# An encoder layer on one core: row sums paused and then run at another pace, decay tables held back, out weights fetched a unit sooner with low weights first, x stored in halves

## The chip, the cores and the metric

The kernel runs on one core of a Trainium2 chip. Its time is the device time of one execution in microseconds (us). Three executions took 1106.18, 1106.75 and 1107.64 us; the median, 1106.75, is the time before. A change of less than about 0.2% of that can't be told from none.

The engines in the text: PE is TensorE (matrix multiplications and transposes), DVE is VectorE, ACT is ScalarE, POOL is GpSimd, SP is SyncE, which issues almost all DMA transfers. Each works through its own queue in order.

## What is computed

One encoder layer for two sequences of 512 rows of 1024 numbers, called the prompt (b = 0) and the sample (b = 1), in float32:

```
mod = silu(c) @ w_ada + b_ada                    # six vectors: sh1, sc1, g1, sh2, sc2, g2
h = rms_norm(x) * (1 + sc1) + sh1
q_a, k_a, v_a, q_r, k_r, v_r, g_r = split(h @ w_in)
o_a = windowed_attention(q_a, k_a, v_a, sink)    # 8 heads of 64, |t - s| <= 128, 2 key/value heads
o_r = silu(g_r) * group_norm(retention(q_r, k_r, v_r, decays))   # 4 heads of 128, both directions
x = x + g1 * (concat(o_a, o_r) @ w_out)
h = rms_norm(x) * (1 + sc2) + sh2
x = x + g2 * (square(relu(h @ w_mlp1)) @ w_mlp2)
y = rms_norm(x, final_g)
```

## The kernel before

**Precision and the matmul.** PE multiplies in a rounded 32-bit format (fp32r). Every operand is split: a high part, rounded by ACT (`split_high`, line 93), and a low part, the difference, taken by DVE (line 101). A product is then three matmuls: high by high, high by low, low by high. In tile names the letters `wh` and `wl` stand for the high and the low part of a weight, followed by the matrix: `rv`, `rq`, `rk`, `rg` for the retention's values, queries, keys and gates, `wo` for the out projection. `mm3_late` (lines 131, 132 and 134) issues the three for a group of banks at once, with the third, the one that needs the late operand, at the end of the group. For the out projection the late operand is the low weight.

**Stages.** The first 48 us are a front whose order is written out by hand: loads, the first modulation vectors, the first norm, and the projections of the prompt's attention. Then come lists of units. A unit loads one weight tile (`load`, always one unit ahead of its use) and multiplies (`use`). `run_units` walks a list. After each group of matmuls a unit yields, and between the two the scheduler of the kernel (`between(rate)`) lets other work in: pieces of attention and retention for which the operands are ready (the `rate` says how many), and, at the pace `clock[3]`, one step of `background_mods`. The lists in order: the prompt's retention values (4 units) and its four retention heads (3 units each), the sample's attention, values and heads, the prompt's out projection (8 units: two halves `hf` of the output columns, four slices `kq` of the input), the sample's out projection, and from 511 us on the MLP's products.

**The background.** 60 row sums on DVE (line 178, `reduce_unit`): a 128 by 1024 tile of w_ada times the activated condition vector, which lies in the tile `cb`, summed along the row. They give the parts of `mod` that the front has not computed: those of the sample's first norm, then gates and the second norm's. Each has its place in DVE's queue fixed behind the last instruction before it. What is left of them when the prompt's out projection has been issued is run in one go (`while background`).

**The late pool.** Then `mixer.close()` gives the memory of one pool (`cb`, attention's and retention's tables) free, and the pool `late` is opened on it. The sample's out projection takes its low weights `wl_wo` from `late` (three buffers), its high weights from the ordinary weight buffers. Both were stored to DRAM by the prompt's units (`kept_wo`, line 110) and are loaded from there (line 119).

**The out projection's end.** For each of four row tiles `t` the product `po_hf_t` is multiplied by the gate (`go`, line 782) and added to x (line 783). The tile x is loaded when the first half is done (line 780) and, when the second is, stored to the DRAM tensor `x2s` (`store`, line 728) for the layer's end; its squares are summed (line 723), and it is scaled in place by its norm's factor (lines 742 and 744), for which the store has to have read it. PE then transposes it (`px`, line 268). In a name such as po_1_3 the first number is the half, the second the row tile; the last number of a name is a running number and means nothing.

**The decay tables.** `decay_table` (line 529 and the two behind it) makes a 128 by 896 table for each retention head of the prompt: ACT scales a table of distances, DVE takes a minimum, ACT exponentiates. It is needed by the first score block of that head; two buffers take turns.

**What sets the order.** Within the lists a scheduler places instructions by their operands and by the order in which the program issues them; two helpers bind it: `issue_after(i)` keeps what follows behind instruction i on its engine, and `keep_in_program_order` keeps a transfer behind the ones that the program issued before it.

## Time and profile before

| what | value |
|---|---|
| median of three executions | 1106.75 us (1106.18 to 1107.64) |
| the profiled execution | 1105.71 us, of which the span of the records is 1103.9 us |
| granted clock of TensorE | 0.998 of full speed, mean |
| PE busy | 1078.9 us (98%) |
| DVE busy | 864.6 us (78%) |
| ACT busy | 515.9 us (47%) |
| moved by DMA | 232.73 MB, 211 GB/s on average |

In a profile row of the timeline the first number is the start and the second the duration in us, then engine, line, operation, the tile written, an arrow and the tiles read, then shapes; what stands in square brackets is how long the engine had been idle before and what ended that. Rows of the waits view read: engine, its operation and line, what it waited for; then total, number of times and the longest. SPq is SP's queue: a row is the issue of a transfer, not its duration. Matmul records overlap: one of 128 by 512 lasts 0.39 us in the records, and the next starts 0.227 us after it.

### The profile page before, as it was taken

What the parts mean: (1) busy time and instruction counts of PE and PEld (TensorE: products, weight loads), DVE (VectorE), ACT (ScalarE), POOL (GpSimd) and SP (SyncE); (2) the same over time, 40 slices, a digit from 0 to 9 for tenths busy, and PEclk for the clock granted to TensorE, in tenths of its full rate; (3) what the DMA queues carried; (4) which work ended last, traced back from release to release, by engine and by line L of the source; (5) the groups of instructions that cost most, each with busy time, mean ns of one, the idle gap of its engine ahead of it and who ended that gap; (6) DMA issues with size and microseconds to landing.
All of it is one profiled execution on the core that took longest, in us unless ns stands there. A gap on an engine that the chain in (4) does not pass through costs nothing.

```text
span 1103.9 us, 14022 instructions
## 1 busy us (share of the span) xinstructions
PE 1078.9 (98%) x5021; PEld 888.9 (81%) x5021; DVE 864.6 (78%) x1448; ACT 515.9 (47%) x885; POOL 49.0 (4%) x55
## 2 busy tenths in 40 slices
PE   7999999999999999999999999999999999999997
PEld 5777788778888788888888888888788888888886
DVE  7979989877887787889878777886659754589786
ACT  6576666545653433574333343333443733335342
POOL 1000000000000001000000000000000000002213
PEclk9999999999999999999999999999999999999999
DMA  9889698765545698734546444452883556525504
GB/s 374 334 301 322 248 379 289 234 194 176 181 139 191 233 360 300 274 123 139 189 169 198 155 162 166 169 181 105 307 322 106 187 194 203 198 77 191 191 19 153
DMA packets 86746, 232.73 MB, mean 211 GB/s; under 512 B 8578, under 2 KB 20882, under 8 KB 86676
## 3 DMA queue, kind: packets, MB, share of 16 engines
q1 hardware_dynamic: 86084, 231.25, 60.2%
q8 instruction: 39, 0.64, 0.2%
q10 hardware_dynamic: 432, 0.57, 0.1%
q14 instruction: 31, 0.25, 0.1%
q0 software_dynamic: 160, 0.02, 0.0%
HBM read 160.75 MB, written 71.06 MB: 210 GB/s over the span
## 4 chain that ended last, share of the span: by engine, by line
PE 87%; DVE 8%; ACT 2%; DMA 1%; issue 1%; POOL 0%; POOLq 0%; ACTq 0%; DVEq 0%
PE x L1350 16%; PE px_None L933 15%; PE y L1350 12%; PE py_None L933 11%; PE po L132 3%; PE po L134 3%; PE po L131 3%; PE po L393 2%; PE ppt L386 2%; PE psc L360 1%; PE pj_rq L131 1%; PE pj_rq L132 1%; PE pj_rq L134 1%; PE pj_rg L134 1%; PE pj_rk L132 1%; PE pj_rk L131 1%
## 5 line engine op out<-in xcount | busy, mean ns | idle before, releaser
L1290 DVE TENSOR_TENSOR uc_l<-ur,uc_h 128x1024 fp32r<-128x1024 f32 x56 | 68.4, 1221 | 53.1 <-ACT uc_h L1290 36.0
L1350 PE MATMUL x<-wc_h,uc_h 128*128 128x512 f32 (+1 forms) x264 | 100.9, 383 | 0.7 <-ACT adacc L246 0.7
L1350 PE MATMUL x<-wc_l,uc_h 128*128 128x512 f32 (+1 forms) x264 | 101.0, 383 | 0.0
L1350 PE MATMUL x<-wc_h,uc_l 128*128 128x512 f32 (+1 forms) x264 | 101.0, 383 | 0.0
L1290 ACT CAST uc_h<-ur 128x1024 fp32r<-128x1024 f32 x56 | 58.9, 1051 | 77.3 <-PE x L1350 25.1
L1350 PE MATMUL y<-wc_h,uc_h 128*128 128x512 f32 x192 | 74.7, 389 | 0.0
L1350 PE MATMUL y<-wc_l,uc_h 128*128 128x512 f32 x192 | 74.7, 389 | 0.0
L1350 PE MATMUL y<-wc_h,uc_l 128*128 128x512 f32 x192 | 74.7, 389 | 0.0
L1290 ACT CAST wc_h<-w 128x1024 fp32r<-128x1024 f32 x48 | 50.5, 1051 | 48.1 <-PE x L1350 24.7
L1290 DVE TENSOR_TENSOR wc_l<-w,wc_h 128x1024 fp32r<-128x1024 f32 x48 | 58.6, 1220 | 17.6 <-ACT wc_h L1290 13.8
L1350 PEld LDWEIGHTS x<-wc_h,uc_h 128*128 128x128 f32 x264 | 49.6, 188 | 10.9 <-ACT adacc L246 1.2
L1350 PEld LDWEIGHTS x<-wc_h,uc_l 128*128 128x128 f32 x264 | 49.6, 188 | 9.8
L1350 PEld LDWEIGHTS x<-wc_l,uc_h 128*128 128x128 f32 x264 | 49.6, 188 | 9.6
L131 PE MATMUL po<-wh_wo,ms 128*128 128x512 f32 x128 | 50.2, 396 | 0.0
L132 PE MATMUL po<-wh_wo,ms 128*128 128x512 f32 x128 | 49.8, 392 | 0.1
L178 DVE CUSTOM_DVE_ANT_0 jka_b<-raw_adat,cb,cols 128x1024 bf16<-128x1024 f32 x38 | 48.2, 1279 | 0.1
L838 ACT CAST wc_s4h<-raw_w 128x1024 fp32r<-128x1024 f32 x16 | 16.8, 1052 | 63.1 <-PE px_None L933 54.1
L370 ACT ACTIVATE st<-st,negm 128x256 f32<-128x256 f32 (+1 forms) x64 | 35.2, 554 | 15.6 <-DVE negm L365 15.6
L1350 PEld LDWEIGHTS y<-wc_h,uc_l 128*128 128x128 f32 x192 | 36.0, 188 | 7.5
L1350 PEld LDWEIGHTS y<-wc_h,uc_h 128*128 128x128 f32 x192 | 36.0, 188 | 7.5
L1350 PEld LDWEIGHTS y<-wc_l,uc_h 128*128 128x128 f32 x192 | 36.0, 188 | 7.5
L933 PE MATMUL py_None<-hch,wc_a 128*128 128x512 f32 x120 | 39.7, 389 | 0.0
(378 smaller groups left out, 2954.8 us busy)
## 6 DMA issues: line engine op xcount, KB each, us to landing
ur<-spill SPq DMA_DIRECT2D x56, 512.0 KB, 4.5
raw_adat<-in_w_ada_t_dram SPq DMA_DIRECT2D x36, 512.0 KB, 6.9
raw_w<-in_w_mlp_dram SPq DMA_DIRECT2D x32, 512.0 KB, 3.5
spill<-s SPq DMA_DIRECT2D x64, 256.0 KB, 3.7
w<-in_w_mlp_dram SPq DMA_DIRECT2D x32, 512.0 KB, 5.2
spill<-u SPq DMA_DIRECT2D x48, 256.0 KB, 2.0
raw_ada<-in_w_ada_t_dram SPq DMA_DIRECT2D x12, 512.0 KB, 9.3
x<-in_x_dram SPq DMA_DIRECT2D x12, 512.0 KB, 7.2
```

Of the source, the lines that this page charges most:

```text
L131: nc.tensor.matmul(ps, lhs[0], rhs[0], start=start, stop=False)
L132: nc.tensor.matmul(ps, lhs[late], rhs[1 - late], start=False, stop=False)
L134: nc.tensor.matmul(ps, lhs[1 - late], rhs[late], start=False, stop=stop)
L178: nc.vector.tensor_tensor_reduce(junk(f"jka_{name}_{sec}_{kc}_{b}"), t, cb[:, b, :], 1.0, bcol[:, sec * KC + kc:sec * KC + kc + 1] if bias ...
L360: nc.tensor.matmul(psc[:, :w], qs[hh][:, isl], k_[:, s, j0 * P:j1 * P], start=(s == 0), stop=(s == 1))
L370: nc.scalar.activation(st[hh][:, :w], st[hh][:, :w], AF.Exp, bias=negm[:, hh:hh + 1], scale=0.125, accum_out=den[:, hh:hh + 1])
L386: nc.tensor.transpose(pt[:, hh * P:(hh + 1) * P], st[hh][:, jj * P:(jj + 1) * P], ident)
L393: nc.tensor.matmul(po, va[:, j0 + jj, g].rearrange("p s e -> p (s e)"), pts[jj][:, s, :], start=(jj == 0 and s == 0), stop=(jj == nj - 1 a ...
L838: nc.scalar.copy(hi, src)
L933: self.last = nc.tensor.matmul(bank[:, cs], x[:, k, :], y, start=first and k == 0 and i == 0, stop=last and k == 3 and i == 2, skip_group_ ...
L1290: last_split[:] = [nc.scalar.copy(hi, src), nc.vector.tensor_sub(lo, src, f(hi))]
L1350: nc.tensor.matmul(out, left[n][x][:, i, ts_], right[n][y][:, i, cs], start=first and i == 0 and k == 0, stop=end and i == 1 and k == 2, s ...
```

## The change

Five pieces:

1. The first ACT instruction of a decay table is held behind the ACT instruction issued last before it.
2. The first `run_units` starts with pace 0.0, and a hook behind its fourth unit sets the pace to 0.8 (it was 0.7 from the start). So no row sum runs beside the four value units.
3. The sample's list of units and the prompt's out projection become one list, run at rate 1.3 (the out projection was a list of its own at rate 1.0). So the first out weight is loaded during the last retention unit.
4. In the sample's out projection `mm3_late` issues the low weights' matmuls first instead of last.
5. The sample's x tiles are stored in two halves, each right behind its own add into x.

```diff
--- before.py
+++ after.py
@@ -125,13 +125,18 @@
         nc.tensor.matmul(ps, lhs[0], rhs[1], start=False, stop=False)
         nc.tensor.matmul(ps, lhs[1], rhs[0], start=False, stop=stop)
 
-    def mm3_late(groups, late):
-
-        for ps, lhs, rhs, start, _ in groups:
-            nc.tensor.matmul(ps, lhs[0], rhs[0], start=start, stop=False)
-            nc.tensor.matmul(ps, lhs[late], rhs[1 - late], start=False, stop=False)
-        for ps, lhs, rhs, _, stop in groups:
-            nc.tensor.matmul(ps, lhs[1 - late], rhs[late], start=False, stop=stop)
+    def mm3_late(groups, late, low_first=False):
+
+        def low():
+            for ps, lhs, rhs, start, stop in groups:
+                nc.tensor.matmul(ps, lhs[1 - late], rhs[late], start=start and low_first, stop=stop and not low_first)
+        if low_first:
+            low()
+        for ps, lhs, rhs, start, stop in groups:
+            nc.tensor.matmul(ps, lhs[0], rhs[0], start=start and not low_first, stop=False)
+            nc.tensor.matmul(ps, lhs[late], rhs[1 - late], start=False, stop=stop and low_first)
+        if not low_first:
+            low()
 
 
     ident = const.tile([P, P], F32, name="ident")
@@ -526,7 +531,8 @@
             return dt
         dt = mwork.tile([P, TW], F32, tag="dtab", name=f"dtab_{b}_{h}", bufs=2)
 
-        nc.scalar.activation(dt, dl, AF.Copy, scale=lg[:, 0, h:h + 1])
+        with tc.issue_after(last_of(mybir.EngineType.Activation)):
+            nc.scalar.activation(dt, dl, AF.Copy, scale=lg[:, 0, h:h + 1])
         nc.vector.scalar_tensor_tensor(dt, dl, nlb[:, h:h + 1], dt, ALU.mult, ALU.min)
         nc.scalar.activation(dt, dt, AF.Exp)
         nc.sync.dma_start(kept_tables[h], dt)
@@ -723,9 +729,9 @@
             nc.scalar.activation(junk(f"jk2_{b}_{hf}_{t}")[:, :512], x2[t][:, hf * 512:(hf + 1) * 512], AF.Square,
                                  scale=D ** -0.5, accum_out=ss[t][:, hf:hf + 1])
 
-        def store(t):
+        def store(t, cs=slice(0, D)):
             r0 = b * S + t * P
-            nc.sync.dma_start(x2s[r0:r0 + P, :], x2[t])
+            nc.sync.dma_start(x2s[r0:r0 + P, cs], x2[t][:, cs])
 
         def scaled(t):
 
@@ -770,7 +776,7 @@
                     banks[hf] = [(mm_bank if t < 3 else aux_bank)(f"po_{b}_{hf}_{t}") for t in range(NT)]
                 for ts_ in ((0,), (1,), (2,), (3,)) if kq == 3 else ((0, 1), (2, 3)):
                     mm3_late([(banks[hf][t], [ms[k][:, i, t * P:(t + 1) * P] for i in range(2)],
-                               (w[0][:, k, :], w[1][:, k, :]), kq + k == 0, kq + k == 4) for t in ts_ for k in range(2)], 1)
+                               (w[0][:, k, :], w[1][:, k, :]), kq + k == 0, kq + k == 4) for t in ts_ for k in range(2)], 1, b == 1)
                     if ts_[-1] == 1:
                         yield
                 if kq == 3:
@@ -781,8 +787,9 @@
                         g_ = f2(f"go_{b}_{hf}_{t}")
                         nc.vector.tensor_tensor(g_, banks[hf][t], gr[hf], ALU.mult)
                         nc.vector.tensor_tensor(x2[t][:, hs], x2[t][:, hs], g_, ALU.add)
+                        if b == 1:
+                            store(t, hs)
                         if hf == 1 and b == 1:
-                            store(t)
                             squares(hf, t)
                             if t > 0:
                                 scaled(t - 1)
@@ -1196,13 +1203,12 @@
     units = first_v
     for h in range(RH):
         units = units + ret_units(hT[0], 0, h)
-    run_units(units, 1.3, {7: lambda: extra.append(norm_x1())})
+    run_units(units, 1.3, {3: lambda: clock.__setitem__(3, 0.8), 7: lambda: extra.append(norm_x1())}, 0.0)
     units = attn_units(hT[1], 1) + ret_v_units(hT[1], 1)
     for h in range(RH):
         units += ret_units(hT[1], 1, h)
-    run_units(units, 1.3)
-    units, norm2_0 = out_units(0)
-    run_units(units, 1.0)
+    more, norm2_0 = out_units(0)
+    run_units(units + more, 1.3)
     flush()
     while background:
         tick_background()
```

How this moves instructions is shown at three places. The changed kernel's lines are numbered a little higher: 183 for 178, 734 for 728, 786 for 780, 788 and 789 for 782 and 783, 767 for 761; 136, 137 and 132 are the high, the middle and the low matmul of `mm3_late`, which were 131, 132 and 134.

**DVE beside the value units.** Names: `jka_b` is a background row sum, `wl_rq_0` the first query weight's low part, `rv_0` to `rv_3` the copies that free the banks of the values. Before:

```order
L178 ISA jka_b_1_1_844,mod_s_89<-raw_adat_755,cb,cols 128x1024
...
L401 TENSOR_TENSOR mix_0_575<-po_0_1_846,otmp_0_1_853 64x2x128 x2
L362 ISA st_0_2_0_874,mx_0_2_878<-psc_0_2_0_879,bias_t,sink_92 128x384
...
L178 ISA jka_b_3_1_871,mod_a_87<-raw_adat_842,cb,onep 128x1024
...
L362 ISA st_0_2_1_875,mx_0_2_878<-psc_0_2_1_883,bias_t,sink_92 128x384
...
L101 TENSOR_TENSOR wl_rq_0_915<-raw_rq_0_912,wh_rq_0_914 128x1024
...
L298 TENSOR_TENSOR rv_0_927<-pj_rv_0_620,rv_0_927 128x512
...
L298 TENSOR_TENSOR rv_1_936<-pj_rv_1_621,rv_1_936 128x512
L298 TENSOR_TENSOR rv_2_983<-pj_rv_2_622,rv_2_983 128x512
L298 TENSOR_TENSOR rv_3_992<-pj_rv_3_623,rv_3_992 128x512
```

Now:

```order
L406 TENSOR_TENSOR mix_0_575<-po_0_0_781,otmp_0_0_786 64x2x128 x2
L101 TENSOR_TENSOR wl_rq_0_899<-raw_rq_0_896,wh_rq_0_898 128x1024
L303 TENSOR_TENSOR pt_0_1_0_795<-ppt_0_1_0_790,pt_0_1_0_795 128x512
...
L303 TENSOR_TENSOR rv_0_911<-pj_rv_0_620,rv_0_911 128x512
L367 ISA st_0_2_0_858,mx_0_2_862<-psc_0_2_0_863,bias_t,sink_92 128x384
...
L406 TENSOR_TENSOR mix_0_575<-po_0_1_835,otmp_0_1_842 64x2x128 x2
...
L303 TENSOR_TENSOR rv_1_920<-pj_rv_1_621,rv_1_920 128x512
```

The row sums are gone from between them, the weight's low part stands ahead of attention's copies (`pt`), and `rv_1` follows without a sum in front of it.

**DVE, SP and PE between the two out projections.** DVE at the end of the prompt's out projection before (the first two rows are the last two row sums, `ms` splits the mixed heads for the sample, `bn` are the last head's statistics, `mix_3` its gated result):

```order
L178 ISA jka_b_7_0_4271,mod_s_90<-raw_adat_4194,cb,cols 128x1024
...
L178 ISA jka_b_7_1_4297,mod_s_90<-raw_adat_4194,cb,cols 128x1024
...
L761 TENSOR_TENSOR ms_0_0_4402<-mix_0_2246,ms_0_0_4402 128x512
L761 TENSOR_TENSOR ms_0_1_4405<-mix_0_2246,ms_0_1_4405 128x512
...
L444 BN_STATS bn_3_0_4322<-pyn_3_4316 128x6
...
L782 TENSOR_TENSOR go_1_0_4372<-po_1_0_4170,gate_0_512_4230 128x512
...
L782 TENSOR_TENSOR go_1_3_4381<-po_1_3_4173,gate_0_512_4230 128x512
L783 TENSOR_TENSOR x_0_2_4142<-x_0_2_4142,go_1_2_4378 128x512
L783 TENSOR_TENSOR x_0_3_4147<-x_0_3_4147,go_1_3_4381 128x512
L460 SCALAR_TENSOR_TENSOR mix_3_3647<-pyb_3_4384,rg_3_3854 128x512
```

Now:

```order
L183 ISA jka_b_6_1_4360,mod_s_90<-raw_adat_4227,cb,cols 128x1024
...
L788 TENSOR_TENSOR go_1_0_4374<-po_1_0_4186,gate_0_512_4242 128x512
...
L788 TENSOR_TENSOR go_1_3_4383<-po_1_3_4189,gate_0_512_4242 128x512
L767 TENSOR_TENSOR ms_2_0_4482<-mix_2_3190,ms_2_0_4482 128x512
L789 TENSOR_TENSOR x_0_3_4156<-x_0_3_4156,go_1_3_4383 128x512
L183 ISA jka_b_7_0_4386,mod_s_90<-raw_adat_4323,cb,cols 128x1024
...
L183 ISA jka_b_7_1_4388,mod_s_90<-raw_adat_4323,cb,cols 128x1024
...
L739 SCALAR_TENSOR_TENSOR v_0_0_4443<-ss_0_0_2111 128x1
```

The last two row sums have moved from ahead of the `ms` rows to behind the last add into x. SP at the same place, before (`raw_w` is a weight of the MLP):

```order
L869 DMA raw_w_0_0_4540<-in_w_mlp_dram 128x1024
L119 DMA wl_wo_0_0_4400<-kept_wo_0_3895 128x1024
L119 DMA wh_wo_0_0_4398<-kept_wo_0_3895 128x1024
L119 DMA wh_wo_0_1_4408<-kept_wo_1_3966 128x1024
...
L728 DMA x2s<-x_0_0_4132 128x1024
L728 DMA x2s<-x_0_1_4137 128x1024
L728 DMA x2s<-x_0_2_4142 128x1024
L728 DMA x2s<-x_0_3_4147 128x1024
```

Now:

```order
L119 DMA wh_wo_0_0_4398<-kept_wo_0_3885 128x1024
L119 DMA wh_wo_0_1_4408<-kept_wo_1_3970 128x1024
L876 DMA raw_w_0_0_4540<-in_w_mlp_dram 128x1024
L734 DMA x2s<-x_0_0_4141 128x1024
L734 DMA x2s<-x_0_1_4146 128x1024
L734 DMA x2s<-x_0_2_4151 128x1024
L734 DMA x2s<-x_0_3_4156 128x1024
L119 DMA wl_wo_0_0_4400<-kept_wo_0_3885 128x1024
```

The load of `wl_wo_0_0` has moved from ahead of the four stores of x to behind them. PE, from the last matmuls of the prompt's out projection to the first of the sample's, with what they wait for, before:

```order
L134 MATMUL po_1_3_4173<-wl_wo_1_3_4279,ms_3_0_4013 128x512
L134 MATMUL po_1_3_4173<-wl_wo_1_3_4279,ms_3_1_4016 128x512
L459 MATMUL pyb_3_4384<-ident,ryn_3_4338 128x128 [waits Activation_49] x4
L131 MATMUL po_0_0_4418<-wh_wo_0_0_4398,ms_0_0_4402 128x512 [waits DMAHW5_49,DVE_49]
L132 MATMUL po_0_0_4418<-wh_wo_0_0_4398,ms_0_0_4402 128x512
...
L134 MATMUL po_0_0_4418<-wl_wo_0_0_4400,ms_0_0_4402 128x512 [waits DMAHW4_49,DMAHW7_49,DMAHW1_49,DMASW0_49]
L134 MATMUL po_0_0_4418<-wl_wo_0_0_4400,ms_0_1_4405 128x512
```

Now:

```order
L132 MATMUL po_1_3_4189<-wl_wo_1_3_4305,ms_3_0_4022 128x512
L132 MATMUL po_1_3_4189<-wl_wo_1_3_4305,ms_3_1_4025 128x512
L132 MATMUL po_0_0_4418<-wl_wo_0_0_4400,ms_0_0_4402 128x512 [waits DMAHW2_49,DMAHW0_49,DMAHW5_49,DMASW0_49,DVE_49]
L132 MATMUL po_0_0_4418<-wl_wo_0_0_4400,ms_0_1_4405 128x512
L132 MATMUL po_0_1_4419<-wl_wo_0_0_4400,ms_0_0_4402 128x512
...
L136 MATMUL po_0_0_4418<-wh_wo_0_0_4398,ms_0_0_4402 128x512 [waits DMAHW3_49]
```

The low matmuls of `po_0_0` and `po_0_1` have come to the front, and the transposes `pyb_3` that stood between the two projections are placed further ahead, among the matmuls of the unit before.

**SP in the middle of the sample's out projection.** The four x tiles are loaded and later stored here, between the loads of the second half's weights. Before:

```order
L780 DMA x_1_0_4644<-in_x_dram 128x1024
L780 DMA x_1_1_4649<-in_x_dram 128x1024
L780 DMA x_1_2_4654<-in_x_dram 128x1024
L780 DMA x_1_3_4659<-in_x_dram 128x1024
L119 DMA wh_wo_1_1_4684<-kept_wo_1_4232 128x1024
L119 DMA wl_wo_1_1_4686<-kept_wo_1_4232 128x1024
L119 DMA wh_wo_1_2_4750<-kept_wo_2_4282 128x1024
...
L253 DMA gate_1_512_4754<-gates 128x512
L119 DMA wl_wo_1_3_4801<-kept_wo_3_4345 128x1024
L119 DMA wh_wo_1_3_4799<-kept_wo_3_4345 128x1024
...
L728 DMA x2s<-x_1_0_4644 128x1024
```

Now:

```order
L786 DMA x_1_0_4644<-in_x_dram 128x1024
...
L734 DMA x2s<-x_1_0_4644 128x512
L786 DMA x_1_1_4650<-in_x_dram 128x1024
...
L734 DMA x2s<-x_1_1_4650 128x512
L786 DMA x_1_2_4656<-in_x_dram 128x1024
L734 DMA x2s<-x_1_2_4656 128x512
L786 DMA x_1_3_4662<-in_x_dram 128x1024
L119 DMA wl_wo_1_3_4805<-kept_wo_3_4345 128x1024
L734 DMA x2s<-x_1_3_4662 128x512
L258 DMA gate_1_512_4758<-gates 128x512
L119 DMA wh_wo_1_3_4803<-kept_wo_3_4345 128x1024
```

The four loads of x stood together; each of the last three now follows the half store of the tile before it, and `wh_wo_1_3` stands behind the last of these stores.

## The prediction

> **What bounds the kernel now.** The page comes first: TensorE (PE) is busy almost all of the span.
>
> ```profile
> span 1103.9 us, 14022 instructions
> PE 1078.9 (98%) x5021; PEld 888.9 (81%) x5021; DVE 864.6 (78%) x1448; ACT 515.9 (47%) x885; POOL 49.0 (4%) x55
> ```
>
> The change leaves the matmuls as many as they are, so it can only shorten or lengthen PE's 25 us of idle time. The list of PE's waits says who owns them (time in total, times, longest):
>
> ```profile
> PE pyb L459 <- ACT ryn L454: 2.5, 2, 1.3
> ...
> PE pj_rg L134 <- DVE wl_rg L101: 1.6, 1, 1.6
> PE px L268 <- ACT x L742: 1.5, 1, 1.5
> ...
> PE pj_rq L131 <- DVE rv L298: 1.2, 1, 1.2
> PE py L124 <- ACT rsc L418: 1.0, 1, 1.0
> ...
> PE pj_rv L131 <- DVE qs L338: 0.8, 1, 0.8
> PE pj_rv L131 <- DVE ks L311: 0.8, 1, 0.8
> PE py L933 <- ACT wc_a L838: 0.7, 1, 0.7
> ```
>
> These eight groups, 10.1 us, are all that the change can win; the other waits lie in the hand-ordered front or at the switch between the MLP products, neither of which it touches. After 511 us nothing moves. One stretch has no idle time at all, and it is the one in which the second out projection runs (columns: stretch, length, busy time of PE, PEld, DVE, ACT, POOL, then clock, DMA share, GB/s):
>
> ```profile
> 420.00:470.00 50.00, 50.00 (x241) 41.44 (x240) 38.69 (x72) 19.83 (x42) 3.39 (x5) 1.00 0.81 292
> ```
>
> What is lost there is lost in full.
>
> **Piece 1: decay tables held back.** ACT's timeline at the start of the values:
>
> ```profile
> 52.62 0.95 ACT L531 ACTIVATE dtab<-dtab 128x896 f32<-128x896 f32 x1 [0.95 <-DVE dtab L530]
> 53.48 0.56 ACT L308 CAST ks<-first 64x512 fp32r<-64x512 f32 x1
> ...
> 55.14 0.96 ACT L531 ACTIVATE dtab<-dtab 128x896 f32<-128x896 f32 x1
> ```
>
> Two exponentials stand ahead of the copies that both pj_rv waits (0.8 + 0.8) end on. They go elsewhere: between nothing and 1.6 us is won. I take 1.0, since DVE's chain of seven subtractions behind the copies stays.
>
> **Piece 2: the pause.** VectorE (DVE) runs row sums of 1.28 us between the work PE waits for (DVE's timeline twice, with PE's line between):
>
> ```profile
> 86.72 1.28 DVE L178 CUSTOM_DVE_ANT_0 jka_b<-raw_adat,cb,onep 128x1024 bf16<-128x1024 f32 x1
> ...
> 89.61 1.22 DVE L101 TENSOR_TENSOR wl_rq<-raw_rq,wh_rq 128x1024 fp32r<-128x1024 f32 x1
> ...
> 91.49 1.88 DVE L298 TENSOR_TENSOR rv<-pj_rv,rv 128x512 fp32r<-128x512 f32 x3
> ```
>
> ```profile
> 91.56 0.50 PE L131 MATMUL pj_rq<-h,wh_rq 128*128 128x512 f32 x1 [1.20 <-DVE rv L298]
> ```
>
> ```profile
> 133.46 1.27 DVE L178 CUSTOM_DVE_ANT_0 jka_b<-raw_adat,cb,cols 128x1024 bf16<-128x1024 f32 x1
> 134.66 0.08 DVE L178 DVE_READ_ACCUMULATOR2_ANT mod_s<- 128x1 f32 x1
> 134.66 1.22 DVE L101 TENSOR_TENSOR wl_rg<-raw_rg,wh_rg 128x1024 fp32r<-128x1024 f32 x1
> ```
>
> In the new order three sums fewer stand ahead of the first rv copy and five fewer ahead of this wl_rg, about 6 us of DVE work: more than either wait. I take both in full, 1.2 + 1.6 = 2.8 (0 to 2.8, as neither need end on DVE alone). The group-norm wait (2.5) is a chain PE, DVE, POOL, DVE, ACT, PE whose length hardly depends on the queue: 0.4 won (0 to 1.4).
>
> The sums still have to be run. At 0.8 instead of 0.7 of one per step the new order stays about three behind to the end, and the last two land where they hurt, in piece 4.
>
> **Piece 3: out projection in one list with the units before.** Its first weight is cast one unit sooner and its first matmuls stand as filler in the last retention head: of the L124 wait of 1.0 I take 0.7 (0 to 1.0).
>
> **Piece 4: low weights first, after the last sum.** This decides. The memory of the late pool is that of the row sums' vector `cb`, so the load of wl_wo_0_0 waits for the last sum. Before, that was no problem:
>
> ```profile
> 418.70 1.28 DVE L178 CUSTOM_DVE_ANT_0 jka_b<-raw_adat,cb,cols 128x1024 bf16<-128x1024 f32 x1
> ...
> 428.77 1.28 DVE L782 TENSOR_TENSOR go<-po,gate 128x512 f32<-128x512 f32 x2
> 429.97 1.28 DVE L783 TENSOR_TENSOR x<-x,go 128x512 f32<-128x512 f32 x2
> ```
>
> ```profile
> 420.06 0.32 SPq L119 DMA_DIRECT2D wl_wo<-kept_wo  x1
> ...
> 428.28 3.47 SPq L728 DMA_DIRECT2D x2s<-x  x4
> 431.84 1.17 SPq L119 DMA_DIRECT2D wh_wo<-kept_wo  x1
> ```
>
> ```profile
> 427.65 0.62 PE L134 MATMUL po<-wl_wo,ms 128*128 128x512 f32 x2
> 428.11 0.60 PE L459 MATMUL pyb<-ident,ryn 128*128 128x128 f32 x4
> ...
> 430.39 0.84 PE L134 MATMUL po<-wl_wo,ms 128*128 128x512 f32 x3
> ```
>
> The sum ended at 420.0, the load went out at 420.06, and PE first read it at 430.39. Now the last two sums stand behind the last x add of the first out projection, the load stands behind the four x stores on SP's queue, and PE's next matmul behind the last po_1_3 is the low one on this very tile; the pyb transposes are placed earlier. So from PE's last po_1_3 matmul (its rows end at 428.27): go, ms and x at 0.60 each (two go in 429.97 - 428.77), then two sums at 1.2: 428.27 + 1.8 + 2.4 = about 432.5, and the load at 432.6. That is the lower bound. DVE also has more to do than PE from head 3's statistics to here (three sums, one wl, five ms, a mix, eight go and x, statistics: 14.7 us, against 51 matmuls at 0.227 and four transposes, 12.0), so it comes 0.9 later: 433.5, at most 434.5. Landing time, from the tile view of wl_wo between 415 and 425 us:
>
> ```profile
> DMA to landing us min/median/max: 3.3/5.6/8.7
> ```
>
> PE is free at 428.1. Stall: at least 432.6 + 3.3 - 428.1 = 7.8, as taken 433.5 + 5.6 - 428.1 = 11.0, at most 434.5 + 8.7 - 428.1 = 15.1. Nothing hides it: PE's queue is in order, and there is no other work in front of it.
>
> A second price hangs on the first. At its end the trace shows what the granted clock does when PE stops (the clock is the third column from the right):
>
> ```profile
> 1096.00:1097.00 1.00, 0.46 (x4) 0.25 (x3) 0.47 (x2) 0.00 (x0) 0.78 (x2) 1.00 0.00 0
> ...
> 1098.00:1099.00 1.00, 0.00 (x0) 0.00 (x0) 0.04 (x1) 0.62 (x2) 0.81 (x2) 0.90 0.10 37
> 1099.00:1100.00 1.00, 0.00 (x0) 0.00 (x0) 0.75 (x1) 0.72 (x1) 0.00 (x0) 0.50 1.01 377
> ```
>
> PE stops at 1096.46 and 2.3 us later the clock is 0.50. So a stall of 8 to 15 us ends at half clock. How long the clock takes to come back no row shows; if it takes the same 2.3 us, PE loses half of that, 1.2 us (0 if at once, 2.3 if twice as long). The Trainium skill (TensorE: Matmul & The Clock Gate, What's actually happening) has the clock back after one busy window of about 3.4 us; by that the loss would be an estimated 1.7 instead of 1.2 and the time 0.5 us longer. The fall to half at 1098.8 agrees with its rule that idle time gates the clock.
>
> **Piece 5: x in halves.** Each x load of the second out projection now stands on SP behind the half store of the x tile before, and that store waits for that tile's add. Three loads run one after the other where four went out together, and wh_wo_1_3 stands at the end of the chain.
>
> ```profile
> 451.62 0.68 DVE L783 TENSOR_TENSOR x<-x,go 128x512 f32<-128x512 f32 x1
> ```
>
> ```profile
> 472.47 0.39 PE L131 MATMUL po<-wh_wo,ms 128*128 128x512 f32 x1
> ```
>
> ```profile
> x<-in_x_dram SPq DMA_DIRECT2D x6, 512.0 KB, 8.4
> ...
> raw_w<-in_w_mlp_dram SPq DMA_DIRECT2D x5, 512.0 KB, 5.0
> ```
>
> First add done at 452.3; three rounds of a load (5.0 as raw_w, since they no longer come in fours) and 1.1 for add and issue, then 5.0 for wh_wo itself: 475.6. Its reader stood at 472.5; without the 0.7 wait before it, and with eight low matmuls (1.8) and 24 small ones (2.9) that now go first, it stands at 476.5. With loads of 8.4 the chain ends at 485.8. So nothing to 9.3 is lost; the quick end is nearer, and I take 1.0. The 0.7 wait on wc_a goes (0 to 0.7), as ACT and DVE catch up during piece 4's stall. The px wait of 1.5 gets a smaller last store, but some of those small matmuls that covered it have left: 0 (1.5 won to 1.7 lost).
>
> **Sum.** Lost 11.0 + 1.2 + 1.0 = 13.2; won 1.0 + 2.8 + 0.4 + 0.7 + 0.7 = 5.6; net +7.6. The profiled execution took 1105.71 us, 1.04 below the median of the runs and 0.5 below the lowest; 1105.71 + 7.6 = 1113.3, and between that and the median's 1114.4 I say **1113.5 us**.
>
> **Rivals.** (a) Not slower: DVE's backlog is behind every one of the eight waits, so the pause wins 9.0 (all but the half of the group-norm chain that is POOL and ACT), while DVE, now ahead, starts the last sums on time and the load lands like the fastest, a stall of 7.8 with a clock that returns at once: 1105.71 - 9.0 + 7.8 = 1104.5. It decides once the stall is below what is won. For it: up to 6 us of DVE work are moved away. Against: the px and wc_a waits hang on transfers and ACT. (b) The x chain becomes a bound beside the stall: the loads land at 8.4 each and wh_wo_1_3 is late by 9.3 instead of 1.0, 1121.6. For it: 8.4 is what this stretch shows; against: those came four at once. (c) The load doesn't wait, the late tile getting memory that is free sooner: then only 5.6 - 0.7 - 1.0 counts (the wc_a wait stays without the stall), 1101.8. Against it: in the order the load names a wait on DVE and stands behind the stores. (d) The change wins nothing, each removed wait being replaced by the next on its chain: 1105.71 + 13.2 = 1118.9.
>
> **Chances.** Forecast 0.67, (a) 0.10, (b) 0.10, (c) 0.05, (d) 0.08. Changes within 0.2% (2.2 us) can't be told from none. (a) falls half on each side of that line, (c) is faster, and the low tail of the forecast gives 0.03 to same and 0.01 to faster: faster 0.11, same 0.08, slower 0.81. The range 1105 to 1120 leaves out (c), half of (a), the top half of (b) and little else; the forecast's own is 1109 to 1118.
>
> **What would show it.** PE waiting 8 to 15 us on the DMA of wl_wo at about 425 us, the load issued behind the x stores and right after the last L178, and a clock of 0.5 for some us behind the wait; the waits of pj_rq, pj_rg and pj_rv gone; a wait on wh_wo near 475. I am wrong if PE's first low matmul of the second out projection has no wait over 5 us, or if the eight waits above stay as they are.

## The result

The change makes the kernel slower. The median of its runs is 1133.18 us (1131.48 to 1135.65) against 1106.64 us for the kernel before on the same chip, a ratio of 1.0237 with a 95% interval of 1.0221 to 1.0254. The prediction was 1113.5 us and a range of 1105 to 1120: the direction is right, the size is not.

The profiled execution took 1135.65 us, the longest of the six and 2.5 us above their median, so what its trace adds up to is somewhat more than what the medians differ by. The head of its page shows that the work is the same (the same 5021 matmuls) and that TensorE (PE) idles more:

```profile
span 1133.9 us, 14028 instructions
PE 1092.0 (96%) x5021; PEld 895.4 (79%) x5021; DVE 865.0 (76%) x1448; ACT 516.2 (46%) x885; POOL 51.2 (5%) x55
```

The list of PE's waits (total us, times, longest), to be held against the one in the prediction:

```profile
PE po L132 <- DMA wl_wo<-kept_wo: 10.1, 1, 10.1
PE py L124 <- ACT rsc L423: 5.2, 4, 2.3
PE pyb L464 <- ACT ryn L459: 3.0, 4, 1.1
PE px L273 <- ACT x L748: 2.9, 2, 2.1
...
PE px L273 <- DVE xl L746: 0.9, 1, 0.9
...
PE pj_rv L136 <- DVE qs L343: 0.7, 1, 0.7
```

The stall on the low output weight that was predicted stands at its head. The waits of pj_rq and pj_rg are gone as predicted; those of pj_rv, which were to go as well, have only shrunk, from 0.8 + 0.8 to 0.7 + 0.3. But L124 rsc (rsc is a score block of the retention behind its decay; four waits of up to 2.3 instead of one of 1.0) and the px transposes have grown, and these were costed at next to nothing.

To place every microsecond I compare the start of the same-numbered PE instruction in both traces: how much later is the n-th PE instruction of the change than the n-th of the kernel before? This lateness is worked out from some 5000 rows, so no single row carries it, and as the order of the matmuls differs a little it can be off by about 1 us inside a stretch. At the end it must be 1135.65 - 1105.71 = 29.9, and it is (the lines are rounded).

| stretch of the kernel before (us) | predicted | lateness gained |
|---|---|---|
| up to 140 (values, first retention weights) | -3.8 | -3.1 |
| 140 to 260 (retention heads of the prompt) | -0.4 | **+16.4** |
| 260 to 418 | 0 | -1.7 |
| 418 to 450 (between the out projections) | +11.5 | +14.0 |
| 470 to 490 (end of the second out projection) | +0.3 | **+4.9** |
| the rest | 0 | -0.5 |
| sum | +7.6 | +29.9 |

The first and the fourth line are close to what was predicted; the second is the miss, and the fifth adds to it. Three runs of the next section (early_sums, no_low and no_half there) issue the same instructions in the same order as the change up to 390 us, and gain 14.2, 14.5 and 15.4 between 140 and 260: a figure of this table is good to about 2 us from one execution to the next. One row of the windows view carries the miss, of before and then of after (stretch, length, busy time of PE, PEld, DVE, ACT, POOL, then clock, DMA share, GB/s):

```profile
140.00:260.00 120.00, 117.48 (x556) 95.49 (x555) 100.32 (x217) 69.15 (x135) 6.53 (x6) 1.00 0.78 263
```

```profile
140.00:260.00 120.00, 108.84 (x471) 84.50 (x471) 92.54 (x185) 62.73 (x110) 6.85 (x5) 0.96 0.78 259
```

In the same 120 us PE gets through 471 matmuls instead of 556, VectorE (DVE) through 185 instructions instead of 217. PE, DVE and ACT are all less busy than before: they wait for one another more, and the clock has dropped in places.

The stall of piece 4 reads row for row as the prediction described it (timeline of SP, DVE and PE between 440 and 452 us):

```profile
440.24 4.53 SPq L734 DMA_DIRECT2D x2s<-x  x4
...
444.34 1.28 DVE L183 CUSTOM_DVE_ANT_0 jka_b<-raw_adat,cb,cols 128x1024 bf16<-128x1024 f32 x1
...
445.54 1.28 DVE L183 CUSTOM_DVE_ANT_0 jka_b<-raw_adat,cb,cols 128x1024 bf16<-128x1024 f32 x1
...
446.89 0.80 SPq L119 DMA_DIRECT2D wl_wo<-kept_wo  x2
...
451.62 0.77 PE L132 MATMUL po<-wl_wo,ms 128*128 128x512 f32 x1 [10.08 <-DMA wl_wo<-kept_wo]
```

The last two row sums end at 446.8, the load goes out at 446.89, PE takes it up at 451.62 after 10.1 us. Behind it the clock is down (windows of 1 us):

```profile
452.00:453.00 1.00, 1.00 (x3) 0.74 (x3) 0.56 (x1) 0.00 (x0) 0.00 (x0) 0.50 0.97 344
...
456.00:457.00 1.00, 1.00 (x4) 0.79 (x3) 0.00 (x0) 0.00 (x0) 0.00 (x0) 0.50 1.06 416
457.00:458.00 1.00, 1.00 (x6) 0.81 (x5) 0.00 (x0) 0.00 (x0) 0.00 (x0) 0.90 0.94 373
```

From 451.62 to about 457.2 PE runs at half clock: 5.6 us, of which half, 2.8, is lost.

### The profile page after: what moved, and what is told of

Same layout as the page of the kernel before. It is cut to its first block, busy times and chain, and to the rows that moved or that the text cites. A ratio compares the mean times of both kernels' runs of the same rounds, so it can differ in the third digit from the quotient of the medians.

```text
span 1133.9 us, 14028 instructions
## 1 busy us (share of the span) xinstructions
PE 1092.0 (96%) x5021; PEld 895.4 (79%) x5021; DVE 865.0 (76%) x1448; ACT 516.2 (46%) x885; POOL 51.2 (5%) x55
## 4 chain that ended last, share of the span: by engine, by line
PE 79%; DVE 12%; ACT 3%; DMA 3%; issue 1%; POOL 1%; SPq 0%; POOLq 0%; ACTq 0%; DVEq 0%
PE x L1356 15%; PE px_None L940 14%; PE y L1356 12%; PE py_None L940 11%; DVE jka_b L183 2%; PE po L398 2%; PE po L137 2%; PE psc L365 2%; PE po L136 2%; PE ppt L391 2%; PE po L132 2%; PE pj_rv L132 1%; PE pj_rv L136 1%; PE pj_rv L137 1%; DVE jka_f L183 1%
## 5 line engine op out<-in xcount | busy, mean ns | idle before, releaser
L137 PE MATMUL po<-wh_wo,ms 128*128 128x512 f32 x128 | 51.2, 400 | 0.3 <-DVE ms L767 0.3
L136 PE MATMUL po<-wh_wo,ms 128*128 128x512 f32 x128 | 51.2, 400 | 0.2 <-ACT ms L766 0.2
L132 PE MATMUL po<-wl_wo,ms 128*128 128x512 f32 x128 | 37.1, 405 | 10.1 <-DMA wl_wo<-kept_wo 10.1
```

The costliest lines, as they stand in the source:

```text
L132: nc.tensor.matmul(ps, lhs[1 - late], rhs[late], start=start and low_first, stop=stop and not low_first)
L136: nc.tensor.matmul(ps, lhs[0], rhs[0], start=start and not low_first, stop=False)
L137: nc.tensor.matmul(ps, lhs[late], rhs[1 - late], start=False, stop=stop and low_first)
```

## The experiments

The five pieces of the prediction are called here hold (1, tables), pause (2), merge (3), low (4) and halves (5). Each run is given with the interval of its ratio to the kernel before on the same chip. Four questions are asked in turn: which piece costs what, why the pause costs, why the held tables cost, and what the merged list, the low weights and the halves do.

### Which piece costs what

**The held tables alone** (only_hold): the kernel before with the two lines of piece 1.

> The kernel before with the held decay tables alone. Theory (two separate losses; the one between 150 and 260 us comes from the held tables, whose stores kept_t stand at the head of SP's queue and wait for ACT, so that the loads of raw_adat and xt behind them go out late): about 1106.6 - 0.6 (values start sooner) + 12 = 1118, with PE waits on rsc and h between 150 and 260 us and an SP wait on the dtab exponential of over 3 us. Rival (that loss comes from the row sums resumed at 0.8): within 1 us of 1106.

Measured: 1110.10 us, ratio 1.0029 (1.0020 to 1.0038), 3.2 us slower, where piece 1 was to win 1.0. Both expectations missed, but the sign speaks against the prediction. Lateness: -0.85 at 140 us (the gain is there, 0.8), +4.5 at 260, 3.8 at the end.

**The pause alone** (only_pause): `run_units(units, 1.3, {3: pace 0.8, 7: ...}, 0.0)` in the kernel before.

> The kernel before with the pause and the pace 0.8 alone. Theory: the waits on rv and wl_rg go (-2.8); the last sums come behind the last x add, so PE waits for wl_wo_0_0 although its high matmuls come first: about 8 us, and 2 to 3 us of half clock behind it: 1106.6 - 2.8 + 10.5 = 1114. Rival (the loss between 150 and 260 us is the pause's as well): 1126.

Measured: 1120.36 us, 1.0119 (1.0104 to 1.0134), between the two expectations. Lateness: -2.4 at 140, +6.1 at 260, +6.8 at 418, +14.8 at 450. So the pause loses twice, 8.5 between 140 and 260 us and 8.0 between the out projections, and wins 2.4.

**Everything but the tables (no_hold), everything but the pause (no_pause)**:

> The changed kernel without the held decay tables. Theory: the waits between 150 and 260 us fall back to those of before, 12 to 15 us less: 1133.2 - 13 = 1120. Rival: 1133.

> The changed kernel with the row sums at 0.7 from the start. Theory: the wait of 10 us on wl_wo and its 3 us of half clock go, the waits on rv and wl_rg (2.8) come back: 1133.2 - 13.4 + 2.8 = 1122.6, and the waits between 150 and 260 us stay. Rival (they are the pause's): 1110.

Measured: 1129.18 us, 1.0205 (1.0185 to 1.0225), without the tables and 1117.48 us, 1.0092 (1.0075 to 1.0109), without the pause. In lateness between 140 and 260 us the change had gained 16.4; without the tables it is 8.1, without the pause 5.3. With either gone about the other is left (8.5 for the pause alone, -0.85 to 4.5 = 5.4 for the tables alone); their sum, 13.9, lies just below the 14.2 to 16.4 of the four traces that hold both, so nothing shows that they cost more together than apart. Without the pause the lateness from 418 to 450 falls from 14.0 to 2.5: the stall of piece 4 is a child of the pause, as the prediction had it.

The largest loss of the kernel without the pause stands elsewhere: 9.0 us between 470 and 490, where the change loses 4.9. With no stall before it, PE waits there for the weights of the small products (wc_s2h, wc_s2l) and longer for the px transposes, and half clock follows twice, for 3.4 and 6.8 us (rows of its waits from 415 to 530 us):

```profile
PE px L273 <- ACT x L748: 2.7, 2, 2.2
...
PE py L940 <- ACT wc_s2h L845: 1.2, 1, 1.2
...
PE py L940 <- DVE wc_s2l L846: 0.9, 1, 0.9
```

So the stall seems to hide part of what this stretch costs in the change.

### Why the pause costs

Two rows of the change's DVE show what a row sum does when its tile is late, and SP's queue shows why it is late (timeline between 158 and 175 us):

```profile
159.96 0.32 SPq L538 DMA_DIRECT2D kept_t<-dtab  x1
160.33 2.76 SPq L159 DMA_DIRECT2D xt<-in_x_t_dram  x4
163.14 1.46 SPq L88 DMA_DIRECT2D raw_adat<-in_w_ada_t_dram  x2
```

```profile
171.41 1.28 DVE L183 CUSTOM_DVE_ANT_0 jka_b<-raw_adat,cb,onep 128x1024 bf16<-128x1024 f32 x1 [5.48 <-DMA raw_adat<-in_w_ada_t_dram]
172.62 0.69 DVE L421 SCALAR_TENSOR_TENSOR rsf<-prs,dtab 128x512 f32<-128x512 f32 x1
```

```profile
174.01 0.79 PE L124 MATMUL py<-rsc,rv 128*128 128x512 f32 x1 [2.31 <-ACT rsc L423]
175.76 0.80 PE L125 MATMUL py<-rsc,rv 128*128 128x512 f32 x1 [0.96 <-DVE rsc L424]
```

DVE's queue is in order. The sum waits 5.5 us for its tile, whose load stood behind the table's store and the four xt loads; the decay multiplication rsf behind it is therefore late, and PE waits 2.3 + 1.0 for the product of it. In the kernel before no sum waits for a tile between 48 us and the end of the list. The first twelve sums of the list serve only the sample (b = 1), and each has a tile of 512 KB of its own; there the last of them starts at 150 us. Put off by the pause, it starts at 175 us (179 in the change), and they fall among the retention heads and the loads of the sample's first norm. The later sums share a tile between two.

**The pause with tiles fetched two ahead** (pause_ahead) takes this wait away and leaves the rest:

```
-        nxt = load(0)
+        nxt = [load(0), load(1)]
...
-            t, nxt = nxt, load(n + 1)
+            t = nxt.pop(0)
+            nxt.append(load(n + 2))
```

> The kernel before with the pause and the pace 0.8, and each row sum's weight tile loaded two sums ahead instead of one. Theory (the sums for the sample's first norm, which need a tile each, now run among retention and hold DVE's queue until their tile lands, 2.9 us in the run of the pause alone): DVE has no wait on raw_adat, the loss between 140 and 260 us falls from 8.5 to about 4, time 1120.4 - 4 = 1116. Rival (it is only that more sums stand in DVE's queue there): 1120.

Measured: 1115.86 us, 1.0083 (1.0068 to 1.0098), 4.0 us less than the pause alone by the two ratios, as the theory said, and the lateness at 260 us falls from 6.1 to 2.0. The waits on tiles are worth about 4 us. The 8 us between the out projections stay (+3.0 at 418, +11.7 at 450): in this kernel, as in the pause alone, PE waits there 4.8 us for the last x tiles, which stand behind the late sums, and not for wl_wo, as was expected of the pause alone.

**The whole change with the last sums early** (early_sums): the pace is raised from the first out unit on, so that the sums are done before the late pool is wanted.

```
-    run_units(units + more, 1.3)
+    run_units(units + more, 1.3, {21: lambda: clock.__setitem__(3, 1.6)})
```

> The changed kernel with the pace raised to 1.6 from the first unit of the prompt's out projection on, so that the last two sums and the load of wl_wo_0_0 stand ahead of the stores of x again. Theory (the tail's wait and the clock behind it cost 13.4): 1133.2 - 13 = 1120, clock 1.00 between 430 and 460 us. Rival (the low weights come too late for a low-first order anyway, or the sums only delay the out projection instead): 1128 or more.

Measured: 1126.91 us, 1.0180 (1.0160 to 1.0200). The stall is gone, as its timeline shows: the last sum starts at 427.05 and the load goes out at 431.01.

```profile
427.05 1.28 DVE L183 CUSTOM_DVE_ANT_0 jka_b<-raw_adat,cb,cols 128x1024 bf16<-128x1024 f32 x1
...
431.01 0.74 SPq L119 DMA_DIRECT2D wl_wo<-kept_wo  x1
```

The lateness from 418 to 450 is 1.1 instead of 14.0. Yet the time falls by 6 only: from 350 to 418 us, where the sums now stand thicker, 2.4 us are lost where the change won 0.9, and 470 to 490 us costs 7.3 instead of 4.9; as I read it, ACT and DVE no longer catch up during a stall there (PE waits 1.0 on wc_s2h and 0.9 on wc_s2l, as without the pause). So 3.3 of the 12.9 gained go to the denser sums and 2.4 to what the stall had hidden.

**The pause with the sums caught up early** (pause_catch): two tiles ahead, 1.1 sums a step from the fourth unit, 0.7 from the eleventh.

```
+    run_units(units, 1.3, {3: pace 1.1, 7: norm_x1, 10: pace 0.7}, 0.0)
```

> The kernel before with the pause beside the four value units, tiles fetched two ahead, then a pace of 1.1 sums a step up to the eleventh unit and 0.7 from there, so that the row sums are only one or two behind the kernel before when the retention starts. Theory: the pause costs because the sums it puts off come back among the retention heads and behind the last x adds; caught up early they do neither, VectorE is on time and the late pool is free as before: 1104 to 1108. Rival: sums that are put off cost wherever they come back, because the stretch up to 140 us has no VectorE time left either: 1110 to 1114.

Measured: 1108.61 us, 1.0025 (1.0015 to 1.0035): neither the theory nor the rival. The loss between the out projections is gone (3.56 at 418, 3.35 at 450), but 140 to 260 us still costs 6.0 (-2.2 to +3.9).

**Six sums left out** (pause_drop and before_drop): the first six of the list are dropped and their results set to 0.5, with the pause and without it.

```
+        for s, kc, _ in todo[:6]:
+            nc.vector.memset((mod_s[0], mod_a[0])[s][:, kc, 1:2], 0.5)
+        todo = todo[6:]
```

> The pause alone with the same six row sums left out, as many as the pause puts off (8 steps x 0.7 = 5.6). Theory: the loss of the pause, 14 us, is the work put off coming back into a stretch where VectorE has no time left (about 8 between 140 and 260 us) and behind the last x adds (about 6); with six sums gone there is nothing that comes back: 1102 to 1107. Rival: the loss is the new order of the loads and of the queues that the pause brings whatever is summed: 1112 or more.

> The kernel before with six of the twelve single row sums of the second sample's first norm left out (their results set to 0.5, so the second sample's output is not the reference's): 6 x 1.36 = 8.2 us less for VectorE and six tiles of 512 KB less. Theory: VectorE is all but full between 89 and 200 us (about 100 of 111 us), so what it is relieved of comes out of PE's waits of 1.2 and 1.6 on it and of part of the group-norm waits: 1102 to 1105. Rival: VectorE's share has no bearing there: 1105.5 to 1107.

Measured: the pause with six sums less takes 1105.89 us, 0.9994 (0.9985 to 1.0004), and the kernel before with six less 1104.26 us, 0.9978 (0.9969 to 0.9988). So the pause loses 13.4 us with these sums and 1.6 without them: nearly all of its cost is the work that comes back (the sums, with the loads of their tiles), and not the rest of the order that it brings. The explanation given with it, that DVE has no time left between 89 and 200 us, is not borne out. The traces count the sums: between 89 and 260 us 27 stand in the kernel before, 27 with the pause, 27 with six left out of either. What differs is which sums stand there and how many come after 418 us:

| row sums that start | 48-89 | 89-260 | 260-418 | after 418 |
|---|---|---|---|---|
| before | 3 | 27 | 29 | 1 |
| pause | 0 | 27 | 26 | 7 |
| pause, six left out | 0 | 27 | 27 | 0 |
| change | 0 | 26 | 26 | 8 |

The times are those of each run, and at 418 us the pause is 6.8 us late and the change 11.5. Counted from the same PE instruction on, five sums are left there with the pause and in the change instead of one, and between 140 and 260 us 22 are run instead of 20.

And PE's waits on DVE that the theory meant to relieve stand unmoved when six sums are gone (kernel before with six less, PE's waits from 48 to 450 us):

```profile
PE pyb L462 <- ACT ryn L457: 1.7, 3, 0.8
PE pj_rg L134 <- DVE wl_rg L101: 1.6, 1, 1.6
PE pj_rq L131 <- DVE rv L301: 1.2, 1, 1.2
```

So 1104.26 us lies in the range of the theory while its main waits did not move; only the group norm's pyb fell, from 2.5 to 1.7. The time alone would have been taken for a proof.

With the pause and six less, the pj_rq and pj_rg waits are gone, and the group norm takes most of it back:

```profile
PE pyb L462 <- ACT ryn L457: 4.4, 3, 2.4
```

That is 2.8 won and 4.4 - 2.5 = 1.9 lost again on pyb. In lateness -2.3 at 140 becomes +0.8 at 260: the gain beside the values is given back, most of it at the group norm, even where nothing comes back.

**The opposite of the pause** (front_load): more sums beside the values, everything computed (tiles two ahead).

```
+    run_units(units, 1.3, {0: pace 1.4, 2: pace 0.3, 3: pace 0.7, 7: norm_x1})
```

> The opposite of the pause, everything computed: the kernel before with tiles fetched two ahead, row sums at 1.4 a step beside the second and third value unit, 0.3 beside the fourth, 0.7 from there: two sums more done by 89 us, none more ahead of the last rv copy. Theory: VectorE is 83% busy between 48 and 89 us and 90% from there to 200 us, so work moved to the front relieves the full stretch: the 1.2 of pj_rq and part of the 1.6 of pj_rg go, 1103 to 1106. Rival: the front is full too (its transfers keep the DMA engines busy, 0.88), and values start late: 1107 to 1109.

Measured: 1106.53 us, 1.0001 (0.9992 to 1.0011). Six sums instead of three are done by 89 us, and nothing is won: +1.0 at 89 us, +2.5 at 140, +2.0 at 260. The time lies between the two expectations. So in these runs neither more nor fewer sums beside the values pay.

### Why the held tables cost

The timeline of the held tables alone, at the first head (the bracket is the idle time before and what ended it):

```profile
147.16 1.03 ACT L530 ACTIVATE dtab<-dl,lg 128x896 f32<-128x896 f32 x1
148.62 1.15 DVE L531 SCALAR_TENSOR_TENSOR dtab<-dl,nlb,dtab 128x896 f32<-128x896 f32 x1
149.81 0.95 ACT L532 ACTIVATE dtab<-dtab 128x896 f32<-128x896 f32 x1 [1.61 <-DVE dtab L531]
...
150.79 0.69 DVE L416 SCALAR_TENSOR_TENSOR rsf<-prs,dtab 128x512 f32<-128x512 f32 x1 [0.95 <-ACT dtab L532]
```

The table stands right ahead of the multiplication that reads it, ACT waits 1.6 us for DVE and DVE 0.95 for ACT, and what is queued behind either waits too. The order is the same at all four heads (147, 161, 198 and 216 us), the waits are not: ACT waits 1.6, 0.3, 2.6 and 1.8 us, DVE for the exponential about 1 us at the first and the last. Before, the tables of heads 0 and 1 were ready at 56 us, and those of heads 2 and 3 some 15 us ahead of their first use. The prediction followed the 1.6 us won and wrote "They go elsewhere". Five runs ask where elsewhere costs.

**The tables' stores on ACT's queue instead of SP's** (hold_act), since xt was issued 8.5 us later with the held tables (164.42 instead of 155.89):

```
-        nc.sync.dma_start(kept_tables[h], dt)
+        nc.scalar.dma_start(kept_tables[h], dt)
```

> The kernel before with the held decay tables alone, but their stores kept_t issued from ACT's queue instead of SP's. Theory (the 5.4 us that the held tables alone lose between 140 and 260 us come from SP standing in front of those stores, 16.4 us of wait in the run of the held tables alone, with the loads of xt and raw_adat behind it): the loss falls to 1 or 2, time 1106 to 1107.5, and the xt loads go out before 160 us instead of at 164.4. Rival (the tables' own work on ACT and DVE in that stretch): 1110.

Measured: 1111.05 us, 1.0035 (1.0021 to 1.0049). Nothing is won; the xt loads still go out at 164.92, now behind other waits of SP. So the stores on SP's queue are not the cause; what the late xt loads cost, this run can't show, as they are still late in it.

**The tables of heads 0 and 1 made at another place** (hold_mid), after the fifth and seventh unit:

> The kernel before with the first decay tables held back, but the tables of heads 0 and 1 are made after the fifth and the seventh unit (about 100 and 120 us) and kept in SBUF, so that neither stands in a retention head's own chain. Theory: the loss of the held tables between 140 and 260 us (about 5 us in the profile) is the two tables' own work in the retention heads, 1.15 us on VectorE and about 2 us of copy and exponential on ScalarE each, with VectorE's queue waiting about 1 us more for each exponential; without it the time is 1105 to 1107 (before less the 0.8 won at the values). Rival: it is the order and the transfers that any held table brings, then 1109 to 1111.

Measured: 1109.70 us, 1.0035 (1.0020 to 1.0049). The loss stays, at another place. The trace has these tables at 116.5 and 137.3 us, and the first's step of 1.15 us on DVE comes in ahead of the wl_rg that PE waits for:

```profile
135.96 1.54 PE L134 MATMUL pj_rg<-h,wl_rg 128*128 128x512 f32 x3 [2.74 <-DVE wl_rg L101]
```

That is 2.7 instead of 1.6, with half clock behind it: +2.5 between 89 and 140 us where the tables held to their heads cost nothing, and 2.0 instead of 5.4 from 140 to 260, with the tables of heads 2 and 3 still held. Out of the heads the loss there shrinks by 3.4, but the place chosen is a bad one.

**The tables held and six sums left out** (hold_drop):

> The held tables alone with the same six row sums left out. Theory: two tables moved into the full stretch cost VectorE 2 x 1.15 us and its waits for the exponentials, less than the 8.2 us that the sums leave free, so the held tables cost nothing any more: 1102 to 1105.5. Rival: the held tables lose by ScalarE and by SyncE's order (their stores and the loads behind them): 1108 to 1111 as without.

Measured: 1109.78 us, 1.0033 (1.0020 to 1.0046), as without. With 8.2 us of DVE work less the loss is as large: the amount of that work is not the cause here, and the theory fell.

**Only heads 0 and 1 held (hold_01), and the same with these two made early (hold_early)**; the last line is in the second kernel alone:

```
+        with tc.issue_after(last_of(ACT)) if h < 2 else ExitStack():
...
+    run_units(units, 1.3, {0: make table 0, 1: make table 1, 7: norm_x1})
```

> The kernel before with only the tables of heads 0 and 1 held back; those of heads 2 and 3 may go as early as their buffers allow. Theory: a held table stands right ahead of its head's first multiplication, a chain of 1.04 (copy), 1.15 (VectorE) and 0.95 us (exponential) in two in-order queues, and each head pays for it, whoever else uses VectorE. So half of the loss of the held tables is left: 1107 to 1109. Rival: the loss comes with heads 0 and 1 alone, whose tables had been made during the values: 1109.5 to 1111.

> The same with the tables of heads 0 and 1 made after the first and the second value unit (about 62 and 72 us) instead of right ahead of their heads; heads 2 and 3 free as before. Theory: no table stands right ahead of its head any more and the first copies of the values are not held up by exponentials either, so nothing of the loss is left and part of the 0.8 at the values is won: 1105 to 1107. Rival: a table costs wherever it is put behind 56 us, because VectorE has nothing left: 1108 to 1110.

Measured: 1110.48 us, 1.0038 (1.0024 to 1.0052), with the two held to their heads; 1106.39 us, 1.0004 (0.9994 to 1.0013), with the two made early (the trace has them at 78.8 to 86 us, somewhat later than expected). So the whole loss hangs on the tables of heads 0 and 1 (the rival of the first run), and on when they are made: made early they cost nothing. The gain at the values is not to be had net either, as the tables then stand in the way of pt copies, for which PE waits 0.7 + 0.3 us there. Holding those of heads 2 and 3 as well costs nothing more here; why the kernel with tables at 116 and 137 us still lost 2.0 there with only these held to their heads stays open. By what path the place costs was not told apart either, neither ACT's waits from DVE's nor both from a rival. PE hardly waits where the tables are read (the multiplications at 150.8 and 164.1 us): with heads 0 and 1 held it stands at 185.6, 187.2 and 198.6 us, for a weight, the group norm and the keys. And in each of the four kernels that lose 5 to 6 us in this stretch (tables held, on ACT's queue, six sums less, heads 0 and 1 alone) xt goes out at 164.4 to 164.9, in the one that loses nothing at 157.0 and in the one that loses 2.0 at 158.7. The first two rows are of the kernel with heads 0 and 1 held, the third of the one with these two made early:

```profile
164.43 2.11 SPq L154 DMA_DIRECT2D xt<-in_x_t_dram  x4
```

```profile
185.59 0.98 PE L134 MATMUL pj_rg<-h,wl_rg 128*128 128x512 f32 x3 [0.84 <-DVE wl_rg L101]
```

```profile
157.04 2.44 SPq L154 DMA_DIRECT2D xt<-in_x_t_dram  x4
```

So the sample's first norm, which comes later with xt, may carry the loss as well as the chain itself; no run holds one and frees the other.

### Merge, low weights first, halves

**The merged list alone** (only_merge):

> The kernel before with the first out projection in one list with the units before it. Theory: the wait of 1.0 us on rsc at about 418 us shrinks by 0.7 and the pace of the row sums stays 0.7 a step, so nothing is late: 1105 to 1107. Rival: casting the first output weight a unit sooner delays the last retention head by the cast and its subtraction, about 2 us: 1108 to 1109.

Measured: 1106.19 us, 0.9999 (0.9990 to 1.0009). The wait on L124 rsc at 418 us is gone, as piece 3 said, but PE's waits from 410 to 475 us now begin with

```profile
PE px L268 <- DVE x L744: 1.1, 2, 0.8
PE pyb L459 <- ACT ryn L454: 0.8, 1, 0.8
```

In lateness 1.6 us are won up to 418 and 2.8 lost up to 450. The 0.7 that the sum counted is not there.

**Everything but low weights first** (no_low):

> The whole change without low weights first. Theory: the stall at about 430 us is the late pool's memory coming free behind the last row sums, so it stays when the high products go first; PE has the eight high products of the first weight tile to do only if that tile has landed, and it is loaded from the same pool behind the low one. So the time stays at 1131 to 1134 (at most 1.8 us shorter). Rival: the order of the products makes the stall, then it goes back towards the 1110 to 1123 that the other parts leave.

Measured: 1.0218 (1.0200 to 1.0235), against 1.0237 (1.0221 to 1.0254) with it: some 2 us less, with intervals that overlap. Its profiled execution, the quickest of its runs, has 8.0 from 418 to 450 us instead of 14.0; so what low first costs lies between 2 and 6 us and is not settled. The stall stays under another name; PE now waits 4.4 us on the last x tiles, whose scaling stands behind the same late sums. So the sums are the cause, as the theory said, but what PE meets first is not the late pool's memory.

**Everything but the halves** (no_half):

> The changed kernel with x stored whole at the end. Theory (the 4.9 us lost behind 470 us in the changed kernel are the half stores' order on SP and the late x loads): 1133.2 - 4.5 = 1128.7. Rival (they come from the low-first order, which takes the cover from in front of the px transposes): 1133.

Measured: 1129.09 us, 1.0204 (1.0189 to 1.0219), as the theory said (1128.7). From 470 to 490 us the lateness changes by -1.15 instead of +4.9. In the change the x tiles come one after another, each load behind the half store of the tile before (SP and DVE between 477 and 490 us):

```profile
477.86 0.32 SPq L734 DMA_DIRECT2D x2s<-x  x1
478.23 0.42 SPq L786 DMA_DIRECT2D x<-in_x_dram  x1
...
482.42 0.69 DVE L789 TENSOR_TENSOR x<-x,go 128x512 f32<-128x512 f32 x1 [0.39 <-DMA x<-in_x_dram]
483.14 0.32 SPq L734 DMA_DIRECT2D x2s<-x  x1
483.51 0.65 SPq L786 DMA_DIRECT2D x<-in_x_dram  x1
...
488.93 0.42 SPq L786 DMA_DIRECT2D x<-in_x_dram  x1
```

This chain is as predicted (a round of 5.3 and 5.4 us, where 6.1 was taken), but no PE row waits for wh_wo_1_3 at its end. What is lost is the cover: of the 48 small matmuls that stand between the last products and the px transposes when x is stored whole, 24 go ahead of those products, and PE waits for the px transposes, 2.9 + 0.9 us as in the list above, then at half clock (the change, and then without halves):

```profile
511.00:520.00 9.00, 7.08 (x38) 6.68 (x39) 4.71 (x9) 5.45 (x10) 0.54 (x1) 0.62 0.08 29
```

```profile
511.00:520.00 9.00, 9.00 (x69) 8.42 (x68) 9.00 (x19) 8.96 (x18) 0.00 (x0) 1.00 0.00 0
```

The halves were left out only together with the stall; what they cost where no stall comes first (9.0 and 7.3 us in the two kernels above, with the low weights first) was not taken apart.

## Why the prediction was right in direction and wrong in size

- **Which stretches can lose.** The step that failed first stands in "What bounds the kernel now": eight groups of waits, 10.1 us, were what the change could win, and only between the out projections was anything held to be exposed ("What is lost there is lost in full"). The reading behind it, "One stretch has no idle time at all", is wrong: from 140 to 200 us the kernel before has none either, as this row of it shows.

```profile
140.00:200.00 60.00, 60.00 (x279) 49.29 (x278) 54.23 (x107) 40.82 (x70) 2.79 (x2) 1.00 0.93 328
```

A stretch that is so full can win nothing and only lose, and 140 to 260 us was costed with a gain of 0.4. It lost 16.4, more than all the rest, 12.9 of it by 200 us.
- **Piece 2, the pause.** "The sums still have to be run ... and the last two land where they hurt, in piece 4" priced their return at the end and not in between. Right: the pj_rq and pj_rg waits went (3.1 won by 140 us with piece 1, predicted 3.8). Wrong: the single-tile sums fall among the heads, and each can hold DVE's queue for its tile (about 4 us, by pause_ahead); the rest of the 8.5 was not split further, beyond 1.9 that returns as group-norm waits. pause_drop shows that all but 1.6 of the pause's 13.4 us hangs on work that comes back. How far the sums fall behind was right: two to four, counted at the same PE instruction, where about three were said.
- **Piece 1, the tables.** 0 to 1.6 won was the whole estimate, with no bound on the other side. The 0.8 was won, though the pj_rv waits did not go, and 5.4 lost in the heads. The work was "elsewhere" exactly in front of what reads it; hold_01 and hold_early show that the place is the cause, and leave open whether the chain or the late xt loads carry it. The order on ACT's queue, where copy and exponential now stand directly ahead of the head, was there to be read before.
- **The group-norm wait** was to shrink from 2.5 by 0.4; it grew to 3.0.
- **Piece 3.** The rsc wait at 418 us goes, but the next wait on the chain takes its place (only_merge: no change): 0.7 was 0.
- **Piece 4** was right in mechanism and nearly in size: 10.1 against 11.0, the load right behind the last sums and the four x stores, as early_sums and no_pause confirm. The load went out 5.35 us after PE had stopped, where 5.4 were worked out, and landed in 4.7 instead of 5.6.
- **The clock** behind the stall was undersized: 2.8 lost, where 1.2 was taken and 2.3 was the upper bound. PE worked 5.6 us before the clock was back: the rest of a 3.4 us stretch and one whole one (last section). The Trainium skill (TensorE: Matmul & The Clock Gate, What's actually happening) asks for one busy window of about 3.4 us and says that the window is free-running. The trace agrees with both; the prediction's estimate of 1.7 from that page left out the part ahead of the window.
- **Piece 5** had the right chain with the wrong victim. Its end, wh_wo_1_3, makes nobody wait; the px transposes do, for which 0 was taken between 1.5 won and 1.7 lost. They cost about 4.9 with the clock, against the 1.0 counted; no_half puts the whole price of halves at about 4 us in the times. The 0.7 wait on wc_a went as predicted; where no stall comes first (no_pause, early_sums) PE waits about 2 us for the other weights of the small products, and the stretch loses 9.0 and 7.3.
- **The rivals.** All four move on the same stretches as the forecast, so none could hold what happened. (b) has the nearest time, 1121.6, and its mechanism, a late wh_wo, did not occur. (d), each removed wait replaced by the next on its chain, holds for piece 3 and in part for the pause.

No version beats the kernel before with everything computed: only_merge, front_load and hold_early are equal to it within 0.2%.

## What to carry to other kernels

Work that is put off must be followed to the place where it comes back, and priced there against the slack of that place; here the stretch with no waits is where it cost most, not least. In an in-order queue the price of a background instruction is not its duration but how late its own operand can be, so ask of each one that moves which load or which other engine it waits for, and who stands behind it. A just-in-time order across two engines, copy, minimum, exponential, reader, makes each engine wait for the other and sends out late what stands behind it; the same work made early cost nothing.
